# Re-dealing layer 1's filler work and asking later for the next layer's modulation weights

## The chip, the cores and the metric

The kernel runs on one core of one Trainium2 chip. A core has five engines with instruction streams of their own: PE (matrix products), DVE and ACT (element-wise work and reductions), POOL (the same, slower, and a DMA queue) and SP (here only a DMA queue). All matrices are fed from on-chip memory (SBUF), products land in PSUM, and everything else comes from device memory (HBM) by DMA. The metric is the device time of one execution in microseconds (us); the median of several runs is compared.

## The reference

Two layers. Each normalises 256 latent and 256 context rows of width 1024, modulates them by vectors computed from `c` and `c_ctx`, multiplies by one wide input matrix, and feeds three mixers side by side: a bidirectional RWKV-7 recurrence, a neighbourhood attention on the 64-wide grid, and a differential attention. Each mixer's output is gated, projected, weighted by a sigmoid gate, and summed; an output product follows.

```
mod_x = silu(c) @ w_mod[l] + b_mod[l]            # shift, scale, gate; the same for c_ctx
hx = rmsnorm(x, g_pre[l]) * (1 + sc_x) + sh_x
zx = hx @ w_in[l]                                # split into the three mixers, gates, merge gates
o  = [rwkv(...), neighbourhood_attention(...), differential_attention(...)] * silu(gates)
y  = sum_n sigmoid(mg_n) * (o_n @ w_branch[l, n]) @ w_out[l]
x  = x + gt_x * rmsnorm(y, g_post[l])            # the context rows too, except in the last layer
```

## The kernel before, in words

Weights come in chunks of 128 x 512 numbers, 256 KB, each one DMA on SP's queue (`chunk`) into one of six `wr` buffers. For accuracy a chunk is split into a rounded part and a rest: ACT writes `wh`, DVE then writes `wl` (`split`), and each product is three matmuls (`mm3`). A dense product of the input matrix (`z_pair`, `z_tok`) takes four such chunks into the PSUM tiles `z` and gives control back after each chunk (`skewed`); with it goes a number, its worth in us as the author's weave counts it: 0.0051 x n per chunk for n token columns and 0.0102 x n for the last one, 2.6 per chunk for `z_tok`. In layer 1, the last, most products have n = 256, so 1.31, 1.31, 1.31 and 2.61; keys and values have n = 512.

The main work of a layer is the recurrence in two segments (`rwkv`: first the context, then the latents) and then attention (`attn`). Each is a generator that gives control back after a unit, with a number that says how much filler it wants beside it. The filler (`fill`) is the layer's dense products in a fixed order: the recurrence's second head group, gates, merge gates (`mgates`), the two attentions' queries, keys and values, gates, more merge gates, and at last the merges of the first two mixers (`merge`). The weave deals them:

```
w = next(main); debt += w
while debt > 0:
    f = next(fill, None)
    if f is None: break
    debt -= f
```

When a unit needs a result that the filler has not made yet, `need` runs the filler on without touching the debt. What is left over at the end of attention runs then; the merge of the third mixer and the output product follow.

The numbers are in `self.yl`, one dictionary for each layer. A pair holds the values of the first and the second segment (for `na` and `diff` the second is for context queries, which layer 1 does not have; for `nd` it is the first and second pair of heads). In the recurrence `G, A, B, C` are the preparations of a head group or pair, `inv` is a triangular inverse on DVE, `q` and `qq` its three and last yields of small products, and `step` one of the four steps of the state in a segment. In attention there are 16 neighbourhood units (`na`), 8 differential ones (`diff`) and two closing units (`nd`). Attention runs as a pipe: unit i's first stage is written beside unit i-1's second, and so on; the closing units have five stages, and while the pipe empties it gives the last unit's number four more times.

The program text is not the order on the chip. When the program is built, the framework's scheduler lines up each engine's instructions: what stands earlier in the text goes first among what has its inputs and buffers ready by the scheduler's own reckoning. Each engine then runs its list strictly in that order.

Layer 0's output product (`outproj`) works through 16 chunks of `w_out`, four for each of four column groups, and after asking for chunk i it calls `ahead(i)`. There the next layer's work is slipped in: the input rows `xs` (tile `k` from `in_xt`), the modulation chunks `ws` (`mod_load(l, ws, n)` asks for chunks until n of 32 have been asked for; tile `k` from `in_wm`, in the slab of 52 buffers), and from i = 7 on two yields of `mod_rows`, each of which multiplies one modulation chunk (PE `y<-k,cs`). After eight chunks of a group `mod_rows` adds the bias row (DVE `k<-y,k`) and turns the row (PE `z<-cst,k`). What of the 32 is not yet asked for after the product is asked for then.

Of the kernel before, what the change touches and what calls it, by code (L numbers as in the profile page):

```python
# [134 lines left out]
class K:  # L135
    def __init__(self, tc, io, out):
        self.tc, self.nc, self.io, self.out = tc, tc.nc, io, out
        self.n = 0
        self.have = {}
        self.in_order = False  # L140

        self.yl = [dict(inv=(57, 42.0), qq=(6, 12.07), step=(6, 6), na=(2.5, 1.19), diff=(2.3, 2.9), q=(1.0, 1.0), nd=(2.75, 5), A=(0, 0), B=(0, 4), G=(0.75, 0), C=(5.6, 7.2)),
                   dict(inv=(23, 51), qq=(3.0, 1.5), step=(6, 6), na=(1.0, 2.3), diff=(4.69, 8.12), q=(1.0, 1.0), nd=(0, 2), A=(0, 0), B=(4.5, 0), G=(0.75, 0), C=(4.0, 6.0))]


    def count(self):
# [1235 lines left out]
    def run(self):  # L1382
        tc, nc, io = self.tc, self.nc, self.io
        with ExitStack() as es:
# [36 lines left out]
            ws = []  # L1421
            self.start(0, P, xs, self.mod_rows(0, P, ws), ws)
            for l in range(L):
                last = l == L - 1
                nq = NX if last else T
                acc = [None] * 8
                PN = None if last else self.params(l + 1)

                def mods():
                    if l == 0:  # L1430
                        yield from self.mod_gate(l, P)
                    if not last:
                        yield from self.mod_gate(l + 1, PN)

                def zs():
                    if l == 0:
                        yield from self.gates(l, nq, 0)
                    if l == 0:
                        yield from self.gates(l, nq, 1)
                        yield from self.rwkv_z(l, P, 1, 0, T, T)  # L1440
                    else:
                        yield from self.rwkv_z(l, P, 1, 0, T, nq)
                        yield from self.gates(l, nq, 1)
                    yield from self.mgates(l, nq, 0)
                    yield from self.attn_z(l, 0, nq)
                    yield from self.attn_z(l, 1, nq)
                    yield from self.gates(l, nq, 2)
                    yield from self.mgates(l, nq, 1)
                    yield from self.mgates(l, nq, 2)

                fill = self.chain(self.both(mods(), zs()), self.merge(l, 0, acc, nq), self.merge(l, 1, acc, nq))
                self.weave(self.rwkv(l, P, last), fill, False)
                self.weave(self.attn(l, P, last), fill)
                self.now(self.merge(l, 2, acc, nq))
                s = self.merged(acc, nq)
                xsrc = io["xt"] if l == 0 else self.xd

                ws, xs, late = [], [], []
                if not last:
                    self.derived(l + 1, PN)  # L1460
                    self.h_new()
                    mod = self.mod_rows(l + 1, PN, ws)

                def ahead(i):
                    if i % 4 == 3 and i // 4 < (2 if last else 4):
                        self.rows_load(xsrc, i // 4, xs)
                    if not last:
                        self.mod_load(l + 1, ws, 2 * i - 4)
                        for _ in range(2 if i > 6 else 0):
                            next(mod)  # L1470

                def rows(t, y, ss):
                    self.residual(t, y, ss, xs[t], last)
                    if not last:
                        self.norm_row(xs[t])

                def done(t, y, ss):
                    if t < 2:
                        rows(t, y, ss)
                    else:  # L1480
                        late.append((t, y, ss))

                self.outproj(l, s, 1 if last else 2, ahead, done)
                if not last:
                    self.mod_load(l + 1, ws, 32)
                    self.now(mod)
                    self.stream_in(PN, xs[0:2], 0)
                    self.start_next(l + 1, PN, NX, (lambda: [rows(*a) for a in late],
                                                    lambda: self.stream_in(PN, xs[2:4], 1)))
                P = PN  # L1490
# [63 lines left out]
```

## Time and profile before

| | us |
|---|---|
| median of 3 runs | 1429.24 (1428.95 to 1432.83) |
| the profiled execution | 1424.81 |
| its span, first to last instruction | 1423.1 |
| PE busy | 1320.4 |
| DVE busy | 995.7 |
| ACT busy | 779.2 |

Busy time is the time in which an engine has an instruction in work; the profile's matmul ends are modelled and matmuls overlap, so a busy PE is not yet a PE at its peak. The granted clock of TensorE has two levels, 1.2 and 2.4 GHz; a window's figure is the share of 2.4 GHz, so 0.50 is the lower level throughout.

### The profile page before, as it was taken

How to read it: one execution, taken by the hardware profiler on the slowest of the kernel's cores; microseconds unless marked ns; L12 is line 12 of the kernel's file. 1: busy time of each engine (PE TensorE's matmuls, PEld its weight loads, DVE VectorE, ACT ScalarE, POOL GpSimd, SP SyncE). 2: the span in 40 equal slices, each digit the busy share in tenths (PEclk: the TensorE clock that was granted, in tenths of full speed). 3: DMA queues.
4: the chain of work that ended last, by engine and by line, in shares of the span. 5: the costliest groups of instructions: out<-in, count | busy, mean ns of one | idle time of the engine just before them, and what ended most of it. 6: DMA issues, size and time to landing. Idle time of an engine off the chain costs nothing. (4 is left out here: it accounts for less than half of the span.)

```text
span 1423.1 us, 28637 instructions
## 1 busy us (share of the span) xinstructions
PE 1320.4 (93%) x10784; PEld 1098.9 (77%) x10784; DVE 995.7 (70%) x2117; ACT 779.2 (55%) x1734; POOL 233.6 (16%) x292
## 2 busy tenths in 40 slices
PE   6998999999999999998999889998999999999897
PEld 4866777889779876677778777888878789867687
DVE  4763469836898368778685386768848893679886
ACT  5462375336863446667433255866449634467653
POOL 0010011012110012224253000101111000122441
PEclk9999999999999999999999999999889999999899
DMA  9466642424324267432545844354513252685454
GB/s 356 129 196 200 208 130 82 128 68 157 119 80 121 77 185 222 155 105 93 178 145 168 324 127 119 113 177 126 170 56 105 68 148 69 182 272 154 141 166 154
DMA packets 112987, 212.42 MB, mean 149 GB/s; under 512 B 13088, under 2 KB 24880, under 8 KB 112848
## 3 DMA queue, kind: packets, MB, share of 16 engines
q1 hardware_dynamic: 102896, 178.33, 40.6%
q0 software_dynamic: 9952, 32.26, 7.0%
q8 instruction: 85, 1.39, 0.4%
q14 instruction: 54, 0.44, 0.1%
HBM read 176.70 MB, written 33.83 MB: 148 GB/s over the span
## 5 line engine op out<-in xcount | busy, mean ns | idle before, releaser
L195 PE MATMUL z<-k,wh 128*128 128x512 f32 (+1 forms) x2352 | 653.9, 361 | 8.8 <-ACT wh L164 4.2
L195 PEld LDWEIGHTS z<-k,wh 128*128 128x128 f32 x2352 | 417.8, 194 | 76.2 <-issue 9.1
L195 PE MATMUL z<-k,wl 128*128 128x512 f32 (+1 forms) x1176 | 421.7, 360 | 7.3 <-DVE wl L185 7.3
L164 ACT ACTIVATE wh<-wr 128x512 fp32r<-128x512 f32 x376 | 235.4, 630 | 317.8 <-PE z L195 212.7
L185 DVE TENSOR_TENSOR wl<-wr,wh 128x512 fp32r<-128x512 f32 x376 | 278.5, 747 | 157.7 <-PE z L195 59.9
L195 PEld LDWEIGHTS z<-k,wl 128*128 128x128 f32 x1176 | 227.1, 194 | 42.8 <-DVE wl L185 12.1
L195 PE MATMUL z<-wh,k 128*128 128x256 f32 x736 | 145.1, 291 | 2.6 <-ACT k L164 1.3
L195 PEld LDWEIGHTS z<-wh,k 128*128 128x128 f32 x736 | 119.6, 196 | 5.7 <-DVE k L192 2.1
L195 PE MATMUL z<-wl,k 128*128 128x256 f32 x368 | 106.7, 290 | 0.6 <-DVE wl L185 0.6
L185 POOL TENSOR_TENSOR k<-k,k 64x512 fp32r<-64x512 f32 (+3 forms) x64 | 78.0, 1222 | 154.9 <-ACT k L164 62.1
L164 ACT ACTIVATE gs<-z 128x512 f32<-128x512 f32 (+1 forms) x134 | 66.7, 500 | 53.5 <-PE z L195 44.1
L164 ACT ACTIVATE k<-k 64x256 fp32r<-64x256 f32 (+5 forms) x146 | 74.8, 537 | 32.0 <-POOL k L185 20.3
L185 DVE TENSOR_TENSOR k<-k,k 128x256 fp32r<-128x256 f32 (+5 forms) x134 | 76.0, 580 | 12.0 <-ACT k L164 9.3
L199 PE MATMUL b<-cst,k 128*128 128x128 f32 x368 | 65.1, 286 | 17.6 <-DVE k L189 5.6
L164 ACT ACTIVATE k<-a,s 128x512 f32<-128x512 f32 (+1 forms) x96 | 59.2, 617 | 33.1 <-DVE s L179 32.1
L195 PEld LDWEIGHTS z<-wl,k 128*128 128x128 f32 x368 | 72.2, 196 | 1.4 <-DVE wl L185 1.0
L199 PEld LDWEIGHTS b<-cst,k 128*128 128x128 f32 x368 | 42.9, 144 | 37.6 <-issue 15.0
L164 ACT ACTIVATE k<-b 128x256 f32<-128x256 f32 (+1 forms) x144 | 62.8, 465 | 16.5 <-PE b L199 15.8
L195 PE MATMUL a<-k,k 128*128 128x512 f32 (+1 forms) x192 | 61.1, 404 | 10.0 <-ACT k L164 6.1
L195 PE MATMUL a<-ar,bk 64*128 64x128 f32 (+1 forms) x512 | 51.1, 288 | 9.6 <-ACT Lab L164 8.8
L195 PEld LDWEIGHTS a<-ar,bk 64*128 64x128 f32 x512 | 43.5, 190 | 21.3 <-ACT Lab L164 15.7
L179 DVE TENSOR_REDUCE s<-a 128x1 f32<-128x512 f32 (+1 forms) x96 | 56.4, 588 | 1.2 <-PE a L195 1.0
(175 smaller groups left out, 1899.4 us busy)
## 6 DMA issues: line engine op xcount, KB each, us to landing
wr<-in_wi SPq DMA_DIRECT2D x296, 256.0 KB, 3.1
k<-in_wm SPq DMA_DIRECT2D x64, 256.0 KB, 5.4
wr<-in_wb SPq DMA_DIRECT2D x48, 256.0 KB, 2.6
md<-gs SPq DMA_DIRECT2D x36, 256.0 KB, 2.9
k<-md POOLq DMA_DIRECT2D x36, 256.0 KB, 4.5
wr<-in_wg SPq DMA_DIRECT2D x32, 256.0 KB, 3.4
wr<-in_wo SPq DMA_DIRECT2D x32, 256.0 KB, 4.0
gd<-gs SPq DMA_DIRECT2D x18, 256.0 KB, 3.2
```

The costliest lines, as they stand in the source:

```text
L164: return self.nc.scalar.activation(out=out, in_=in_, func=func, **kw)
L179: return self.nc.vector.tensor_reduce(out=out, in_=in_, axis=AX.X, op=op, **kw)
L185: return (eng or self.nc.vector).tensor_tensor(out=out, in0=a, in1=b, op=op)
L195: return self.nc.tensor.matmul(out, lhsT=lhsT, rhs=rhs, start=start, stop=stop)
L199: return self.nc.tensor.transpose(out, in_, self.ident[0:k, 0:k])
```

## The change

Four numbers of layer 1's dictionary change, in `qq`, `step`, `diff` and `nd`, and with them which dense products stand beside which units. Layer 0's dictionary stays. In `ahead`, the modulation chunks are asked for up to 2i-8 instead of 2i-4.

```diff
-dict(inv=(23, 51), qq=(3.0, 1.5), step=(6, 6), na=(1.0, 2.3), diff=(4.69, 8.12), q=(1.0, 1.0), nd=(0, 2), A=(0, 0), B=(4.5, 0), G=(0.75, 0), C=(4.0, 6.0))
+dict(inv=(23, 51), qq=(0, 1.5), step=(6, 4.5), na=(1.0, 2.3), diff=(5.86, 16.24), q=(1.0, 1.0), nd=(0, 5.0), A=(0, 0), B=(4.5, 0), G=(0.75, 0), C=(4.0, 6.0))
...
                     if not last:
-                        self.mod_load(l + 1, ws, 2 * i - 4)
+                        self.mod_load(l + 1, ws, 2 * i - 8)
                         for _ in range(2 if i > 6 else 0):
                             next(mod)
```

## Rows read from the trace of the kernel before

**Rows 1.** The page, busy time of each engine over the span.

```profile
PE 1320.4 (93%) x10784; PEld 1098.9 (77%) x10784; DVE 995.7 (70%) x2117; ACT 779.2 (55%) x1734; POOL 233.6 (16%) x292
```

**Rows 2.** Windows, layer 0's output product: length, busy, clock, DMA share, GB/s.

```profile
790.00:795.00 5.00, 5.00 (x64) 4.47 (x58) 0.00 (x0) 0.56 (x2) 0.00 (x0) 1.00 1.06 392
...
797.00:802.30 5.30, 0.19 (x2) 0.00 (x0) 2.01 (x4) 1.26 (x2) 0.00 (x0) 0.86 0.99 336
802.30:807.60 5.30, 5.27 (x29) 4.67 (x30) 1.35 (x4) 2.25 (x8) 0.00 (x0) 0.50 1.04 376
```

**Rows 3.** Timeline of PE, layer 0's output product: start, length, [idle before <-releaser].

```profile
793.48 0.64 PE L195 MATMUL y<-k,cs 128*32 128x128 f32 x16
...
796.91 0.28 PE L195 MATMUL z<-wh,k 128*128 128x256 f32 x1
802.33 0.48 PE L199 MATMUL z<-cst,k 128*128 128x128 f32 x1 [5.14 <-DVE k L185]
...
822.08 0.28 PE L195 MATMUL z<-wl,k 128*128 128x256 f32 x1
```

**Rows 4.** Timeline of ACT, layer 0's output product.

```profile
794.44 0.63 ACT L164 ACTIVATE wh<-wr 128x512 fp32r<-128x512 f32 x1 [9.02 <-DMA wr<-in_wo]
...
800.72 0.63 ACT L164 ACTIVATE wh<-wr 128x512 fp32r<-128x512 f32 x1 [1.37 <-DMA wr<-in_wo]
```

**Rows 5.** Timeline of DVE, layer 0's output product.

```profile
801.99 0.28 DVE L185 TENSOR_TENSOR k<-y,k 128x128 f32<-128x128 f32 x1
```

**Rows 6.** Timeline of SP's DMA issues, layer 0's output product.

```profile
773.25 8.49 SPq L167 DMA_DIRECT2D k<-in_wm  x8
...
784.06 4.67 SPq L167 DMA_DIRECT2D k<-in_wm  x8
789.09 0.33 SPq L167 DMA_DIRECT2D wr<-in_wo  x1
...
794.50 0.33 SPq L167 DMA_DIRECT2D wr<-in_wo  x1
...
801.46 4.81 SPq L167 DMA_DIRECT2D k<-in_wm  x8
```

**Rows 7.** The tile view of the modulation chunks, 765 to 830 us.

```profile
DMA to landing us min/median/max: 5.0/5.3/8.9
```

**Rows 8.** Windows, layer 1: last recurrent steps, head of attention, late hole.

```profile
1172.00:1231.00 59.00, 58.00 (x1085) 55.04 (x1086) 28.21 (x39) 25.50 (x45) 4.63 (x3) 0.97 0.36 102
1231.00:1268.00 37.00, 30.93 (x187) 23.51 (x186) 31.17 (x71) 24.29 (x60) 9.33 (x12) 0.91 0.83 249
...
1326.50:1346.00 19.50, 13.21 (x64) 9.33 (x63) 16.11 (x45) 12.78 (x34) 10.00 (x13) 0.82 0.47 149
```

**Rows 9.** Windows behind two short waits of PE in attention.

```profile
1243.50:1246.00 2.50, 2.33 (x8) 1.77 (x8) 2.50 (x3) 1.05 (x2) 2.50 (x5) 0.72 0.75 229
1375.30:1380.00 4.70, 4.20 (x31) 3.82 (x32) 4.70 (x11) 2.38 (x6) 3.06 (x5) 1.00 0.45 121
```

**Rows 10.** Timeline of PE, those two waits.

```profile
1243.53 1.88 PE L195 MATMUL a<-k,k 128*128 128x512 f32 x4 [2.43 <-DVE k L185]
...
1375.35 0.41 PE L199 MATMUL b<-cst,k 128*128 128x128 f32 x2 [2.03 <-DVE k L185]
```

**Rows 11.** Timeline of DVE and PE, steps of the recurrence's second segment.

```profile
1194.51 2.14 DVE L185 TENSOR_TENSOR UV<-ht,PC 64x512 f32<-64x512 f32 x2
...
1200.31 1.15 PE L195 MATMUL a<-UV,k 128*64 128x64 f32 x32
...
1220.19 0.40 PE L195 MATMUL z<-k,wh 128*128 128x256 f32 x2
...
1220.55 0.40 PE L195 MATMUL z<-k,wh 128*128 128x256 f32 x2
```

**Rows 12.** Timeline of POOL, late in the differential units.

```profile
1332.97 3.77 POOL L185 TENSOR_TENSOR k<-k,k 64x256 fp32r<-64x256 f32 x4 [8.93 <-ACT k L164]
1336.68 1.44 POOL L167 DMA_DIRECT2D k<-od  x2
```

More of the change, by code (lines that the diff above doesn't have):

```diff
@@ L142, in __init__ @@
         self.yl = [dict(inv=(57, 42.0), qq=(6, 12.07), step=(6, 6), na=(2.5, 1.19), diff=(2.3, 2.9), q=(1.0, 1.0), nd=(2.75, 5), A=(0, 0), B=(0, 4), G=(0.75, 0), C=(5.6, 7.2)),
-                   dict(inv=(23, 51), qq=(3.0, 1.5), step=(6, 6), na=(1.0, 2.3), diff=(4.69, 8.12), q=(1.0, 1.0), nd=(0, 2), A=(0, 0), B=(4.5, 0), G=(0.75, 0), C=(4.0, 6.0))]
+                   dict(inv=(23, 51), qq=(0, 1.5), step=(6, 4.5), na=(1.0, 2.3), diff=(5.86, 16.24), q=(1.0, 1.0), nd=(0, 5.0), A=(0, 0), B=(4.5, 0), G=(0.75, 0), C=(4.0, 6.0))]
     def count(self):
```

## The prediction

> **What bounds the kernel now.** I read the page first: PE is busy 93% of the span [rows 1]. The change adds no work and takes none away: every matmul, split and DMA is still there, in another order. So the time can only move by idle time of PE and by its clock. I then cut the span into windows and looked for windows where PE is not full, at the two places that the edits touch: layer 0's output product, and everything in layer 1 up to the last product.
>
> In the output product one hole stands out. From 797.0 to 802.3 PE is busy for 0.19 us while the DMA share is 0.99, and in the 5.3 us behind it PE runs at clock 0.50, which is 1.2 GHz instead of 2.4 [rows 2]. The PE timeline shows the hole as one wait of 5.14 us: a row-turn of the next layer's modulation stands ahead of the product's matmuls in PE's queue, and it waits for DVE [rows 3]. DVE adds that modulation row at 801.99 [rows 5], directly behind its half of the split of w_out chunk 13; ACT begins its half at 800.72, as soon as that chunk lands, and had sat idle 9.02 us for chunk 11 [rows 4]. The SP timeline says why chunk 11 is late. It is issued at 789.09, behind eight modulation chunks from 773.25 and eight more from 784.06; chunk 13 goes out at 794.50 [rows 6]. By then the DMA engines are full: share 1.06, 392 GB/s [rows 2]. So this hole is made of bytes that stand ahead of w_out in one full queue.
>
> In layer 1 the weave pours dense products ("pieces", each one weight chunk of 256 KB) between units of the recurrence and of attention. Four stages matter. The last recurrent steps are full of PE work: 58.00 of 59 us. The head of attention is not: 30.93 of 37 us, with DMA share 0.83. Late in the differential units lies a second hole: 13.21 of 19.5 us, mean clock 0.82 [rows 8]. There the gate products are used up and the first merge cannot start, because its loads of od and md stand in POOL's queue behind four subtractions that begin at 1332.97; the loads go out from 1336.68 [rows 12].
>
> **The later modulation chunks.** With 2i-8 instead of 2i-4 the product's steps 3 and 4 ask for nothing, and every later step up to 15 asks for chunks numbered four lower. Ahead of w_out chunk 11 there are then 12 modulation chunks instead of 16, and the remaining ten instead of six are asked for after the product. Issued behind one another, eight such chunks and one change of transfer take from 784.06 to 789.09 [rows 6], 0.63 us each. Bytes give 262,144 B / 376 GB/s = 0.70 us, or 0.78 us at 336 GB/s [rows 2]. I take 0.72 us, so 4 x 0.72 = 2.9 us (2.5 to 3.1). Chunks 11 to 15 all land that much earlier, the row-turn comes that much earlier, and the hole shrinks from 5.1 to about 2.2 us. The gain is not the whole hole, as the w_out chunk still sits behind a full queue. Lower bound 0: the builder could place the row-turn behind a later split. Upper bound 5.1.
>
> By the Trainium skill (DMA: Bandwidth & Descriptors, Specifications) HBM gives one core about 358 GB/s, which would make a chunk 0.73 us and the four 2.9 us; here the trace shows 392 GB/s in one window, so the measurement is above the page's limit, and the sum does not change.
>
> The clock: after the hole the matmuls run at half speed for 5.3 us, which costs half of that, 2.65 us [rows 2]. Shorter gaps disagree: after a wait of 2.43 us the window from 1243.5 has clock 0.72, after one of 2.03 us the window from 1375.3 has 1.00 [rows 9, 10]. A rest of 2.2 us lies between them, so I count 0 and keep 2.65 as the bound of a gain. The Trainium skill (TensorE: Matmul & The Clock Gate, Why this matters for your kernels) asks for no idle gap between bursts of matmuls so that the clock is kept; if the clock were kept here, the sum would be 2.65 us lower, and no row decides it.
>
> What may be late next: the modulation chunks themselves. The first is used at step 7, when six are asked for; from then on two are used and two asked for per step. The lead falls from eight to four, which is two steps of 24 matmuls of 0.12 us [rows 11] plus 16 small ones of 0.64 us together [rows 3], some 3.5 us each; with a landing time of 5.3 us in the middle and 8.9 at most [rows 7] this lead of 7 us holds except for the slowest. The last chunks: now all issued by 806.3 and landed by 815.2 at the latest [rows 6, 7], while PE is in the product until after 822 [rows 3]. Total bytes are unchanged, so they land at the same time, and PE comes for them about 3 us sooner than now, still behind 815. Cost 0; if that cover were gone, the rest of the wait would fall on PE. Layer 1's first weights go out behind them as before.
>
> **The new numbers of layer 1.** I added up the yields. The fill is worth 277.9 in the weave's own units in both kernels. Before, the recurrence asks for 192 and attention for 63.5; after, 183 (3 less in the first segment, 4 x 1.5 less in the second) and 87.9 (8 x 1.17 and 5 x 3 more, as the last unit's value is asked for five times). Following the debt unit by unit, the fill behind the last recurrent step stands five pieces later than before; it stands two pieces later at the fourth and fifth differential units, level at the sixth, and by the end the merges are dealt two to three yields sooner. Nothing was left over before, and nothing is after. A piece is 12 matmuls; three take 0.36 us [rows 11], so 1.44 us a piece, 7.2 us for five.
>
> In the recurrent steps, taking fill away opens no gap: DVE has the next state ready at 1196.65 (1194.51 + 2.14) and PE gets to it at 1200.31 [rows 11], so 3.66 us of fill per step lie behind the chain's own end, and less than 2 us per step goes away. Cost 0, and the steps end up to 7 us sooner. Were the chain longer, each step would idle by what is missing.
>
> The 7.2 us reappear in attention, where PE idles 6.1 us in the head and 6.3 us in the late hole [rows 8]. In the late hole the pieces that matter are the two that are now dealt behind the fourth differential unit: attention is then 2 x 1.44 = 2.9 us further on when the gate products run out, and the wait for POOL's loads is that much shorter. I take 2.9 us; bounds 0 (fill is poured by position only and POOL's order does not change) and 6.3 (hole gone). At the head I take 0: there PE lacked chunks that had landed, not positions; DMA share is 0.83. Bounds there are a loss of 7.2 us (below) and a gain of 6.1 us. The merges dealt sooner end in the same wait for the last norm: 2.03 us [rows 10], 0.
>
> The sum: -2.9 - 2.9 = -5.8 us. The profiled execution took 1424.81 us, which would become 1419.0. It lies 4.4 us under the median of the three runs, 1429.24, on which I put the forecast: 1423.4 us. Within 0.3%, or 4.3 us, a measurement of this kernel does not tell a change from none.
>
> **Rivals.**
> *Only one of the two pays* (chance 0.30). The hole in the product shrinks by 2.9 and layer 1 breaks even, or the row-turn is queued elsewhere and only layer 1 gains: 1429.24 - 2.9 = 1426.3. For it: layer 1's fill is level again before the late hole. Against: both holes are plain to see.
> *Nothing happens in the product*, because SP's order stays (part of the same 0.30). The builder placed chunks 0 to 10 ahead of all modulation chunks, so it goes by readiness, not by text; chunk 11, though, stands exactly in text order. 1426 to 1429.
> *The head of attention starves* (chance 0.14), the one on the slow side. Five pieces move from the steps, where the DMA share is 0.36, to a head where it is 0.83 [rows 8]. Their five weight chunks stand in SP's queue behind attention's own loads. If none can be fed there, 7.2 us of matmuls come after the head instead of beside the steps: +7.2 - 2.9 = +4.3, 1433.5. It decides from 2.9 us of lost cover on, the other gain left out.
> *All of it* (chance 0.12): hole and slow clock in the product go (5.1 + 2.65) and the late hole too (6.3): -14, 1415.
>
> **How the numbers follow.** My forecast (-3.5 to -9 us) has 0.44, all of it 0.12, one half 0.30, the starved head 0.14. Faster by over 0.3%: 0.44 + 0.12 and a little of the halves, 0.58. Within 0.3%: 0.28. Slower: 0.14. The range goes from 1414, near the full gain, to 1432, which takes in the halves and no change, and leaves out only the worse part of the starved head. The likeliest case's own range is 1420 to 1426.
>
> **What would show it.** In the profile after: 12 modulation chunks ahead of w_out chunk 11 on SP; ACT's wait for that chunk about 6 us instead of 9.0; PE's wait before the row-turn near 2 us. In layer 1: recurrent steps shorter by 1 to 2 us each with PE still full, and less idle in the 20 us before the first merge. I am wrong if the row-turn waits as long as before, if PE idles more at the head of attention, or if the late hole only moves.

## The result, and the profile after

| | before | after |
|---|---|---|
| median, us | 1429.1 (4 runs, 1426.55 to 1432.83) | 1415.43 (4 runs, 1410.37 to 1416.04) |
| ratio, 95% interval | | 0.9895 (0.9863 to 0.9926) |
| the profiled execution, us | 1424.81 | 1415.45 |

The changed kernel is faster by 13.7 us between the medians and by 15.0 us (10.6 to 19.6) by the ratio, in which the experiments below are told: about 1%. The time lies inside the predicted range, near its fast end, but the forecast gain was 5.8 us: the sign was right and the size was not.

The page after, span and busy time of each engine:

```profile
span 1413.8 us, 28622 instructions
...
PE 1320.0 (93%) x10784; PEld 1102.6 (78%) x10784; DVE 994.7 (70%) x2117; ACT 778.2 (55%) x1734; POOL 234.1 (17%) x292
```

PE is busy as long as before to 0.4 us [rows 1], so over the whole execution the 9.3 us between the two spans are idle time of PE. That is not yet a reading of the change. PE runs the same matmuls in the same order in both kernels until well into layer 1, and yet the output product's first `w_out` chunk goes out at 745.83 here and at 738.77 in the profile of before: this execution was some 7 us late when it came to the first thing that was changed, 4.8 us of that with PE busy. So stages are compared below, not times from the start.

**The output product.** SP's DMA issues after:

```profile
779.36 0.90 SPq L167 DMA_DIRECT2D k<-in_xt  x2
780.31 2.36 SPq L167 DMA_DIRECT2D k<-in_wm  x4
782.76 1.93 SPq L167 DMA_DIRECT2D k<-in_xt  x2
786.13 6.03 SPq L167 DMA_DIRECT2D k<-in_wm  x8
793.00 0.33 SPq L167 DMA_DIRECT2D wr<-in_wo  x1
...
804.45 7.66 SPq L167 DMA_DIRECT2D k<-in_wm  x12
```

The windows that answer to [rows 2] (around the work ahead of the row-turn, then behind it), then ACT, DVE and PE around the row-turn. The columns of a window are its length, then busy time and number of instructions for PE, PE's weight loads, DVE, ACT and POOL, then the granted clock, the DMA share and GB/s.

```profile
793.30:798.30 5.00, 5.00 (x65) 4.43 (x63) 0.00 (x0) 0.00 (x0) 0.00 (x0) 1.00 1.03 376
800.00:805.30 5.30, 5.16 (x53) 4.62 (x52) 3.09 (x7) 2.33 (x8) 0.00 (x0) 1.00 1.05 383
805.30:810.60 5.30, 5.28 (x59) 4.49 (x63) 2.26 (x7) 2.70 (x10) 0.00 (x0) 1.00 1.01 377
```

```profile
798.39 0.63 ACT L164 ACTIVATE wh<-wr 128x512 fp32r<-128x512 f32 x1 [9.97 <-DMA wr<-in_wo]
...
803.71 0.63 ACT L164 ACTIVATE wh<-wr 128x512 fp32r<-128x512 f32 x1 [1.05 <-DMA wr<-in_wo]
```

```profile
804.98 0.28 DVE L185 TENSOR_TENSOR k<-y,k 128x128 f32<-128x128 f32 x1
```

```profile
805.32 0.33 PE L199 MATMUL z<-cst,k 128*128 128x128 f32 x1 [0.16 <-DVE k L185]
```

Twelve modulation chunks stand ahead of w_out chunk 11, as forecast. ACT still waits 9.97 us for that chunk, but PE no longer waits behind it: 0.16 us where there were 5.14 [rows 3], and the half-speed stretch behind the hole [rows 2] has clock 1.00.

**Layer 1.** Four windows show it, cut at the same instructions in each kernel: from the first segment's first state step to the first scores of attention (the recurrence); to a group of scores late in the differential units; to the first chunk of the last product; to the end. Before, then after:

```profile
1033.66:1243.53 209.87, 198.06 (x2270) 176.58 (x2270) 143.97 (x284) 117.00 (x245) 19.00 (x23) 0.96 0.35 104
1243.53:1323.44 79.91, 74.58 (x482) 59.06 (x483) 69.52 (x143) 56.78 (x147) 23.55 (x28) 0.96 0.67 204
1323.44:1377.30 53.86, 44.31 (x302) 39.33 (x300) 44.31 (x111) 30.23 (x71) 17.82 (x22) 0.90 0.47 142
1377.30:1420.09 42.79, 35.83 (x288) 34.81 (x288) 33.28 (x72) 18.90 (x47) 12.05 (x15) 0.98 0.54 174
```

```profile
1035.81:1235.93 200.12, 190.21 (x2209) 169.99 (x2210) 140.08 (x279) 112.53 (x237) 18.34 (x23) 0.94 0.35 100
1235.93:1312.05 76.12, 72.17 (x478) 59.05 (x478) 68.18 (x143) 56.56 (x146) 24.01 (x28) 0.96 0.68 215
1312.05:1367.78 55.73, 49.61 (x368) 44.84 (x366) 47.85 (x115) 34.65 (x80) 18.39 (x22) 1.00 0.55 171
1367.78:1410.73 42.95, 35.35 (x288) 34.53 (x286) 33.65 (x74) 18.21 (x45) 12.10 (x15) 0.98 0.54 174
```

Read the counts of matmuls first. The recurrence has 61 fewer, which is the five pieces of 12 that the prediction counted, to one at the window's edge; the third window has 66 more. So the fill went where it was said to go. Now the lengths: the recurrence is 9.8 us shorter, while the three windows of attention together are 1.8 us shorter too (176.56 to 174.80), though they hold five pieces more.

One execution of each is thin ground for differences of 2 us, and there are more. PE's order in layer 1 is that of before in e1 and e9 to e12 below, and that of the changed kernel in e2. Over the six executions with the old order the recurrence takes 209.87 to 211.71 us and attention 174.25 to 176.56; over the two with the new one 198.59 and 200.12, and 174.80 and 178.34. On average the recurrence is 11.4 us shorter, attention 1.6 us longer, and the whole 9.8 us shorter.

POOL around the loads of od, to compare with [rows 12]:

```profile
1322.08 4.16 POOL L185 TENSOR_TENSOR k<-k,k 64x256 fp32r<-64x256 f32 x4 [9.24 <-DVE s L179]
1326.19 1.44 POOL L167 DMA_DIRECT2D k<-od  x2
```

The loads still go out straight behind four subtractions, but the fill is no longer used up by then: the last merge gates are stored from 1330.38 on, 4.2 us behind these loads, where that store was 9 us ahead of them (1327.73 to 1336.68). PE's idle time in the 20 us ahead of the first merge falls from 4.8 to 2.7 us.

### The profile page after: what moved, and what is told of

Read it like the earlier page. It is cut to its first block, busy times and chain, and to the rows that moved or that the text cites. A ratio compares the mean times of both kernels' runs of the same rounds, so it can differ in the third digit from the quotient of the medians.

```text
span 1413.8 us, 28622 instructions
## 1 busy us (share of the span) xinstructions
PE 1320.0 (93%) x10784; PEld 1102.6 (78%) x10784; DVE 994.7 (70%) x2117; ACT 778.2 (55%) x1734; POOL 234.1 (17%) x292
## 4 chain that ended last, share of the span: by engine, by line
PE 31%; DVE 14%; ACT 7%; DMA 4%; issue 4%; POOL 1%; SPq 0%; DVEq 0%; ACTq 0%; POOLq 0%
PE z L195 18%; PE a L195 6%; ACT k L164 4%; DVE wl L185 3%; PE y L195 3%; DVE k L185 2%; PE b L199 2%; DVE k L192 2%; DVE X L182 1%; PE b L195 1%; POOL k L185 1%; DVE tmp L185 1%; DVE X L185 1%; DVE s L179 1%; DMA wr<-in_wo 1%
## 5 line engine op out<-in xcount | busy, mean ns | idle before, releaser
L199 PEld LDWEIGHTS b<-cst,k 128*128 128x128 f32 x368 | 42.8, 144 | 40.4 <-issue 17.1
L164 ACT ACTIVATE k<-b 128x256 f32<-128x256 f32 (+1 forms) x144 | 62.7, 465 | 15.7 <-PE b L199 14.9
L195 PE MATMUL a<-k,k 128*128 128x512 f32 (+1 forms) x192 | 58.2, 391 | 5.3 <-DVE k L185 2.4
```

Source lines behind the costliest of these rows:

```text
L164: return self.nc.scalar.activation(out=out, in_=in_, func=func, **kw)
L195: return self.nc.tensor.matmul(out, lhsT=lhsT, rhs=rhs, start=start, stop=stop)
L199: return self.nc.tensor.transpose(out, in_, self.ident[0:k, 0:k])
```

## The experiments

Each kernel was run in five rounds beside the kernel before on the same chip. Where nothing else is said, the baseline is the kernel before, and differences in us are the ratio applied to that chip's median of before (1427.97 for e1 to e4, 1426.62 for e5 to e8, 1426.25 for e9 to e12).

**e1: the modulation edit alone.**

```diff
-self.mod_load(l + 1, ws, 2 * i - 4)
+self.mod_load(l + 1, ws, 2 * i - 8)
```

> The kernel before with the modulation chunks asked for up to 2i-8 and layer 1's numbers left as they were. Theory (bytes ahead of w_out in a full queue): the wait of PE before the row-turn, 5.14 us before, is under 1 us, the half clock behind it is gone, and the time falls by 5 to 8 us (5.0 us of wait and up to 2.65 us of clock). Rival 1 (as predicted, only four chunks of 0.72 us): a wait near 2 us stays, -3 us. Rival 2 (the hole belongs to that one execution, the gain is all layer 1's): within 2 us of before.

Measured: 1422.76 us, ratio 0.9976 (0.9953 to 0.9999), 3.4 us faster (0.1 to 6.7). In its profile PE has no idle time ahead of the row-turn and clock 1.00 behind it, so hole and slow clock are both gone. The wait is as the theory says; the time is below its 5 to 8 us and near rival 1's 3. A hole of 5.14 us was a long one: in the seven other executions with the old order in this product (e2 to e7 and e12) the wait is 2.96 to 4.19 us.

**e2: layer 1's four numbers alone.**

```diff
-qq=(3.0, 1.5), step=(6, 6), ... diff=(4.69, 8.12), ... nd=(0, 2)
+qq=(0, 1.5), step=(6, 4.5), ... diff=(5.86, 16.24), ... nd=(0, 5.0)
```

> The kernel before with layer 1's four numbers changed and the modulation chunks as before. Theory (the two halves touch different stretches and add up to the whole, about -14 us): -6 to -9 us, with the hole of 5 us in the output product still there and PE's idle time in the 15 us before the od loads near 1 us instead of 4. Rival (the product's gain is nearly all): -1 to -3 us.

Measured: 1414.77 us, ratio 0.9910 (0.9892 to 0.9928), 12.9 us faster (10.3 to 15.4): more than any theory gave. The product of the two ratios, 0.9886, is the change's 0.9895 within its interval. The halves add as far as these intervals can tell, and layer 1 is by far the larger one. Both signs that the theory named are there: the wait in the product stays, 3.47 us here, and PE's idle time in the 14 us ahead of the loads of od is 0.6 us, where before has 4.2 in 13 us.

**e3 and e4: the dealing split in two**, the recurrent numbers (`qq`, `step`) in e3, attention's (`diff`, `nd`) in e4, all else as before.

> The kernel before with only qq and step changed: nine units of filler fewer beside the recurrence, attention's numbers as before, so three merge chunks are left for the end. Theory (what pays is filler kept in reserve until the softmax chain of the differential units leaves PE empty): most of the dealing's gain, -5 to -9 us. Rival (attention must also be told to take it): the filler is left over at the end and comes after attention with nothing beside it, 0 to +6 us.

> The kernel before with only diff and nd changed: the recurrence takes its filler as before, attention takes more of it sooner and the merges are all dealt at the last differential unit. Theory (reserve): the gate products run out sooner, so the hole before the first merge is as long or longer, 0 to +5 us. Rival (it is the numbers of attention that fill the holes): -3 to -7 us.

Measured: e3 1415.56 us, ratio 0.9918 (0.9891 to 0.9945), 11.7 us faster (7.9 to 15.6), above its theory's 5 to 9. e4 1433.34 us, ratio 1.0042 (1.0025 to 1.0058), 6.0 us slower (3.6 to 8.3), the side that its theory names, but not because the gate products run out sooner. PE's order in e4 is that of before up to the four transposes in the first line below (1332.58 in before), so up to there the same fill has been dealt. What differs is that the first merge stands next in PE's list, ahead of the last scores. PE, then ACT, then POOL in e4:

```profile
1336.02 0.66 PE L199 MATMUL b<-cst,k 128*128 128x128 f32 x4 [0.92 <-DVE k L192]
1341.84 1.04 PE L195 MATMUL z<-k,wh 128*128 128x256 f32 x3 [5.16 <-ACT k L164]
...
1383.65 1.08 PE L199 MATMUL b<-cst,k 128*128 128x128 f32 x4 [3.85 <-DVE k L185]
```

```profile
1341.37 0.72 ACT L164 ACTIVATE k<-k 128x256 fp32r<-128x256 f32 x2 [3.28 <-DMA k<-od]
```

```profile
1336.40 1.85 POOL L185 TENSOR_TENSOR k<-k,k 64x256 fp32r<-64x256 f32 x2 [8.94 <-ACT k L164]
1338.20 0.72 POOL L167 DMA_DIRECT2D k<-od  x1
```

The merge waits for ACT, and ACT waits for od, which POOL loads behind the first two of its subtractions. So here the prediction's wait for POOL's loads is real: PE waits 5.16 us, and for 3.28 us ahead of its own part ACT stands idle for od. Dealt that soon, the merges are also used up before attention ends, and nothing stands beside the last norm (3.85 us, where before has 2.03 [rows 10]). The last two windows of layer 1 hold as many matmuls as in before, 592 to 590, and 4.5 us more idle time (21.0 to 16.5). With the pieces kept back the same two numbers do no harm: e2 differs from e4 by `qq` and `step` alone, and its first merge waits 0.23 us.

**e5, e6, e7: which pieces, and how many.** e5 has only `qq=(0, 1.5)`, e6 only `step=(6, 4.5)`, e7 a larger dose, `qq=(0, 1.5), step=(6, 3)`.

> The kernel before with only qq=(0, 1.5) in layer 1. e3 showed that the two recurrent numbers alone give nearly all of the dealing's gain; this run and the next split them. Theory A (each piece kept back fills a place in which PE idled or ran at half clock later, and the gains add): two or three pieces are kept, 3 to 6 us faster; the steps of the first segment shorter by about 3 us, those of the second unchanged. Rival B (only what is kept until the differential units pays): 0 to 2 us faster, since the pieces kept in segment 0 are used up in the preparation of segment 1.

> The kernel before with only step=(6, 4.5) in layer 1: four steps of the second segment each ask for 1.5 less. Theory A (gains add piece by piece): 6 to 9 us faster, and with e5 it adds up to e3's 11.7. Rival B (only what is kept until the differential units pays): 10 to 13 us faster by itself, all of e3's gain. Either way the four steps of the second segment are shorter by some 3.6 us in all with PE still without a gap.

> The kernel before with qq=(0, 1.5) and step=(6, 3): a larger dose, 1.5 per step less than e3. Theory (the prediction's 3.66 us of fill behind the chain's end in each step is cover, and e3 has used 0.9 us of it): the steps end another 3.6 us sooner with no gap of PE, and the late hole gets more fill: 12 to 16 us faster than the kernel before. Rival 1 (the cover is used up): PE idles over 1 us in the four steps and the gain falls to 6 to 10 us. Rival 2 (attention has no place left for more fill): steps shorter, but the fill is left over behind attention, so 9 to 12 us faster, no better than e3.

Measured: e5 1420.71 us, ratio 0.997 (0.995 to 0.999), 4.3 us faster; e6 1421.62 us, 0.9961 (0.9944 to 0.9979), 5.6 us faster; together 9.9 against e3's 11.7 (7.9 to 15.6). The gains add as far as these intervals can tell, and neither carries the whole; e6 came out just under its 6 to 9. The profiles show two different ways. In e5 nothing is kept until attention: by the first scores one piece more has been dealt than in before, and the second segment's steps are longer, not unchanged (36.43 us against 34.28). The recurrence still takes only 205.9 us (209.87 in before), with 7.6 us of idle time in it instead of 11.8. So `qq` pays inside the recurrence, where neither theory looked. In e6 the recurrence keeps its idle time (12.1), and attention has 19.4 us of it instead of 21.8. e7: 1414.33 us, 0.9921 (0.9892 to 0.995), 11.3 us faster, no better than e3. Its window over the second segment's steps, from the first to the fourth, shows PE idle 0.46 us where e3 has none in 30.7 us:

```profile
1182.69:1210.60 27.91, 27.45 (x559) 25.30 (x560) 11.73 (x14) 11.19 (x20) 4.63 (x3) 1.00 0.42 114
```

The steps have lost another 2.8 us and are just about to open, and what they give away is paid back: the recurrence is 2.5 us shorter than e3's (198.40 to 195.94), attention's three windows are 4.0 longer (177.46 to 181.46). That is rival 2's time, though not its reason: no more fill is left at the end than in e3 (279 matmuls in the last window of both). It went into the first of the three windows (477 to 518 matmuls), where e3 had only 4.3 us of idle time left to fill.

**e8: the later modulation chunks with e3's dealing**, that is the changed kernel with `diff` and `nd` put back.

> The changed kernel with the two attention numbers put back (diff and nd as before), so the later modulation chunks with e3's dealing. Theory (the halves add, and the attention numbers bring little): 13 to 16 us faster than the kernel before, level with the changed kernel. Rival (the attention numbers deal the first merges two to three yields sooner, which the changed kernel needs with the full reserve): 9 to 12 us, behind the changed kernel by 2 us or more.

Measured: 1414.4 us, ratio 0.9924 (0.9898 to 0.9949), 10.8 us faster: less than the sum of e1 and e3 (15.1), which lies just outside its interval (7.3 to 14.6), and not to be told from the changed kernel, whose interval overlaps. Its middle lies in the rival's range and its interval reaches into the theory's, so e8 does not decide between them. Once layer 1 has its reserve, the two attention numbers buy nothing that these runs can tell.

**e9, e10: the modulation edit turned round and doubled.** e9 asks up to 2i, e10 up to 2i-12.

> The kernel before with the modulation chunks asked for up to 2i instead of 2i-4: the edit of the change turned round, by the same four chunks. Theory (the hole in the output product is made of bytes ahead of w_out in a full queue, 0.72 us a chunk): 20 chunks instead of 16 stand ahead of w_out chunk 11, the row-turn comes 2.9 us later (hole of 6 to 8 us, then half clock), 2 to 5 us slower. Rival (the hole depends on where the scheduler puts the row-turn, not on the chunks ahead): the hole is the same or elsewhere, within 1.5 us of the kernel before.

> The kernel before with the modulation chunks asked for up to 2i-12: four fewer still than the change's 2i-8, a lead of zero to two chunks over their use. Theory (the hole is closed with 2i-8 already, so nothing is left to gain, while each chunk now lands 5 us after it is asked for and PE takes it within 2 to 4 us): PE waits for modulation chunks instead of for w_out, 0 to 5 us slower than e1, that is -3 to +2 us against the kernel before. Rival (the scheduler puts the modulation behind the product's matmuls, so nothing waits): as e1, 3 to 5 us faster.

Measured: e9 1428.58 us, ratio 1.0021 (1.0001 to 1.0041), 3.0 us slower, in its theory's range of time but not with its mechanism. The profile of e9, window ahead of the row-turn (from the first matmul of that column group), then ACT's splits, then PE:

```profile
772.50:800.39 27.89, 23.34 (x234) 21.81 (x232) 8.53 (x17) 7.06 (x23) 0.00 (x0) 0.98 1.03 373
```

```profile
795.40 0.63 ACT L164 ACTIVATE wh<-wr 128x512 fp32r<-128x512 f32 x1 [8.93 <-DMA wr<-in_wo]
...
798.78 0.63 ACT L164 ACTIVATE wh<-wr 128x512 fp32r<-128x512 f32 x1 [2.75 <-DMA wr<-in_wo]
```

```profile
800.39 0.47 PE L199 MATMUL z<-cst,k 128*128 128x128 f32 x1 [4.56 <-DVE k L185]
```

Chunk 11 goes out later, 17.1 us behind the start of its column group instead of 15.5, but the row-turn now stands behind the split of chunk 12 instead of 13 [rows 4, 5], so the wait is 4.56 us and not the 6 to 8 expected. The scheduler's placing matters, as the rival says. From that group to the product's first store (of `xd`) e9 takes 44.0 us, within what the old order shows (41.4 to 44.7), so its profile does not show the 3.0 us, whose interval reaches down to 0.1. e10: 1422.79 us, 0.9983 (0.9959 to 1.0008), 2.4 us faster by its middle and not to be told from e1 or from no change; its profile has no idle time from that group to the row-turn. A lead of nearly nothing still made nobody wait, and not by the rival's way: PE's order is that of before.

**e11: the modulation chunks on POOL's queue**, asked for at 2i-4 as before.

```diff
-ins = self.dma(self.nc.sync, w, ...)
+ins = self.dma(self.nc.gpsimd if slab and not self.in_order else self.nc.sync, w, ...)
```

> The kernel before with the modulation chunks of layer 1 issued on POOL's queue instead of SP's, still asked for at 2i-4; PE's and DVE's orders stay. On SP the w_out chunks then have no modulation chunk ahead of them. Theory (bytes: both queues share the same 16 DMA engines, which are full): w_out chunk 11 goes out sooner but its packets share the engines with the modulation chunks, so it lands 0 to 3 us sooner; the hole stays above 2 us, 0 to 3 us faster. Rival (order on SP alone): chunk 11 goes out as soon as its buffer is free, the hole is gone, 4 to 7 us faster.

Measured: 1419.76 us, ratio 0.9965 (0.9939 to 0.9992), 5.0 us faster (1.1 to 8.7). The window ahead of the row-turn, and the last line of the tile view of the w_out chunks:

```profile
773.21:796.38 23.17, 23.17 (x234) 21.84 (x233) 9.11 (x18) 8.23 (x25) 11.42 (x22) 1.00 1.03 368
```

```profile
DMA to landing us min/median/max: 2.7/5.4/14.9
```

The hole is gone, so the theory of bytes alone falls and the rival holds. Both effects are visible: sharing the full engines stretches the slowest w_out chunk to 14.9 us from issue to landing (6.1 before), but SP issues chunk 11 at 773.8 instead of 789.1, more than enough to cover that.

**e12: od and the first mixer's md loaded from SP's queue** instead of POOL's, layer 1 only; PE's and ACT's instruction orders stay as they were.

> The kernel before with the loads of od and of the first mixer's md in layer 1 issued on SP's queue instead of POOL's; PE's and ACT's orders stay. Theory of the prediction (the late hole is these loads waiting in POOL's queue behind four subtractions that begin at 1333): od is loaded some 5 us sooner, PE's wait of 4 to 6 us ahead of the first merge shrinks by 3 to 5 us, 3 to 5 us faster. Rival 1 (the fill has run out, so the merges that start sooner are only used up sooner and the idle time moves behind them): the wait shrinks, the end stays within 2 us. Rival 2 (SP itself gets to these loads late, behind a weight chunk that waits for its buffer): no change or slower.

Measured: 1425.95 us, ratio 1.0012 (0.9986 to 1.0037): no change. PE around the late hole, before and in e12:

```profile
1330.93 0.73 PE L195 MATMUL a<-k,k 128*128 128x512 f32 x2 [0.69 <-ACT k L164]
1332.58 0.66 PE L199 MATMUL b<-cst,k 128*128 128x128 f32 x4 [0.92 <-DVE k L192]
1335.52 1.22 PE L195 MATMUL a<-k,k 128*128 128x512 f32 x2 [2.28 <-ACT k L164]
...
1343.47 0.63 PE L195 MATMUL z<-k,wh 128*128 128x256 f32 x3 [0.24 <-ACT k L164]
```

```profile
1329.33 0.73 PE L195 MATMUL a<-k,k 128*128 128x512 f32 x2 [0.69 <-ACT k L164]
1330.98 0.66 PE L199 MATMUL b<-cst,k 128*128 128x128 f32 x4 [0.92 <-DVE k L192]
1333.91 1.22 PE L195 MATMUL a<-k,k 128*128 128x512 f32 x2 [2.27 <-ACT k L164]
...
1341.76 0.63 PE L195 MATMUL z<-k,wh 128*128 128x256 f32 x3 [0.23 <-ACT k L164]
```

And SP's issue of od in e12:

```profile
1327.41 1.25 SPq L167 DMA_DIRECT2D k<-od  x2
```

The loads go out 14.4 us ahead of the first merge's matmul (1341.76) instead of 6.8 us (1336.68 to 1343.47), 7.6 us sooner, and not one wait of PE changes. PE waits there for ACT and DVE in the last differential units' own chain, and the merge stands behind those units in PE's list. This experiment leaves the orders of PE and ACT alone. Where the merge does stand further ahead, in e4, the same loads are what PE waits for; early loads together with such an order were not tried.

## Why the prediction came out as it did

**The modulation edit: mechanism and order right, the price of the chunks right, that of the clock too low.** Twelve chunks ahead of chunk 11, as said; from the first row load to chunk 11's issue it takes 13.6 us (779.36 to 793.00), 3.2 less than the 16.8 of before, where the sum had 2.9. But the forecast hole of 2.2 us is closed in this profile, and from the start of that column group to the first store of `xd` the two profiles differ by 7.5 us, while e1 gained 3.4 in the median. The profile of before had caught the longest hole of eight executions with the old order in this product (before, e2 to e7, e12), and of three with the new one (after, e1, e8) e8 still waits 1.56 us. On average over these the row-turn comes 3.1 us sooner (27.2 to 24.1 us behind the start of the group), which is the 2.9 of the sum. The stretch from the row-turn to the store is 1.8 us shorter (15.5 to 13.6), at granted clock 1.00 in all three instead of 0.81 to 0.89: the slow clock went with the hole, and it had been counted 0, with 2.65 as its bound. Together that is 4.9 us (42.6 to 37.7), within e1's interval (0.1 to 6.7). So that the forecast 2.9 comes near e1's 3.4 is partly luck: a term was left out, and the interval is wide. "Bytes that stand ahead of w_out in one full queue" needs both halves: in e11 the engines are as full (DMA share 1.03) and the hole is gone, because the chunks stand in another queue. "ACT's wait for that chunk about 6 us" was wrong (9.97): the chunk is sooner, but so is the end of ACT's earlier work.

**Layer 1: this is the term that was mis-sized: 2.9 us forecast, 12.9 measured (10.3 to 15.4).** The prediction counted the pieces rightly, five fewer in the recurrence, and said that they leave without opening a gap. Then it gave most of that back: "The 7.2 us reappear in attention", of which only the two pieces behind the fourth differential unit were to meet idle time. So the recurrence was to be 7.2 us shorter and attention 4.3 longer. Over the six executions with the old order and the two with the new one it is 11.4 shorter and 1.6 longer. In the recurrence, busy time falls by 9.5 us and idle time by 1.9 (11.9 to 9.9). In attention's three windows the five pieces add 5.9 us of busy time, and idle time falls by 4.3 (22.3 to 17.9). In all 9.8 us: 6.3 of idle time and 3.6 of busy time for the same matmuls. Single pairs of executions give 8.0 to 11.8 us (the two shown above 11.5), and 9.8 lies just under e2's interval, so up to some 3 us of its median are not found in these windows.

So two things failed in that step. First, the idle time: the late part gave 3.4 us (9.55 to 6.12), near the 2.9 forecast, but the recurrence gave 1.9 and the stretch from the first scores on 1.5 (5.7 to 4.2), where the text had 0; the last window took 0.6 back. "At the head I take 0: there PE lacked chunks that had landed" fell only in part: there, from 1243.53 to 1323.44, the number of matmuls stayed (482 to 478), and the gain is small. Second, the price of a piece: 1.44 us is what it costs at full clock. The five pieces took 1.9 us each out of the recurrence and brought 1.2 us each into attention. In the recurrence the clock is part of it: the 16 to 19 us ahead of the second segment's steps, which lose one piece, ran at granted clock 0.60 to 0.68 in seven of the eight executions. In the late window it was 0.90 to 0.94 in the six with 302 matmuls there, and 0.97 and 1.00 in the two with 368, but 0.94 and 0.92 in e3 and e8 with 377, so that fuller stretches run faster isn't shown. The text weighed the clock only in the output product, and never for layer 1. How the 3.6 us of busy time divide between clock and denser packing isn't settled, since the granted clock of one and the same order differs between executions too.

**The late hole's cause was wrong for the order that PE ran.** That "the first merge cannot start, because its loads of od and md stand in POOL's queue" is refuted by e12 for that order. The hole is attention's own chain of ACT and DVE, uncovered when the gate products have run out. The loads do bind in e4, where the merge stands further ahead. The remedy in the sum, more fill left at that place, was nevertheless the right one, and its sign came true: less idle time in the 20 us ahead of the first merge (4.8 us before, 2.7 after, 2.6 in e2).

**What held.** The cover in the recurrent steps: 3.66 us of fill per step, of which the change takes part, and PE has no gap in them; e7, which takes 1.5 per step more, shows the first 0.46 us. The head of attention did not starve: the DMA share of its window is 0.68 against 0.67, and the window is 3.8 us shorter than before's and 1.5 shorter than e12's (79.91, 77.62, 76.12). Neither did "only one of the two pays" come true, as e1 and e2 show, nor did SP's order stay. "All of it", the rival that came nearest with 1415, was right in its time and half right in its reasons: the product's hole and clock went as it says, but in layer 1 the late hole is only smaller (6.1 us of idle time in its window instead of 9.55), and the gain came from several places. That its total fits is luck: it had 7.75 us for the product, where e1 measured 3.4, and 6.3 for layer 1, where e2 measured 12.9.

## What to carry to other kernels

Filler is worth what the place costs in which it is poured: a stretch whose engine is busy to the last microsecond on fill alone can give some away, and the same matmuls cost little in a chain of short waits. Here five pieces made one stretch 11.4 us shorter and the other 1.6 us longer. When work is moved from a full stage to a gappy one, price both ends by their own windows, idle time and clock, instead of carrying one price per piece across. Read a hole in more than one execution before pricing it: 5.14 us here, 2.96 to 4.19 in seven others. And a name at the head of a queue is a suspect, not a cause: the load that stood behind four subtractions could be moved forward by 7.6 us without anybody noticing, and the same load held PE up for some 3 us in an order that asked for it sooner.

## What the hardware showed that was not expected

The granted clock differs between executions of the same instructions, with PE busy throughout. One stretch ahead of the second segment's steps, where e1 and e9 to e12 have before's order, ran as follows before and in e12 (windows; the other four are within 0.2 us of e12):

```profile
1172.99:1188.99 16.00, 15.99 (x339) 15.50 (x341) 6.59 (x8) 5.97 (x10) 0.00 (x0) 0.89 0.19 61
```

```profile
1170.58:1189.68 19.10, 19.05 (x340) 18.52 (x341) 6.63 (x8) 5.97 (x10) 0.00 (x0) 0.64 0.16 52
```

The 3.1 us between them are nearly the whole effect of e1. What sets the clock there wasn't found; in both, PE had idled about 4 us spread over the 45 us of the triangular inverse just ahead.

DMA windows go up to 392 GB/s before [rows 2] and 383 after, above the 358 GB/s that the prediction set beside them. The Trainium skill (Perfetto Trace Analysis, Roofline) says that this figure is one core's share when both cores of a pair stream, and that a core alone can go to about 435; the windows here lie between the two.
